# Zero-padding the keys' second parts to 128 rows in three attentions, and two runs of keys instead of three in the first

## The chip, the core and the metric

The kernel runs on one core of one Trainium2 chip. The metric is the device time of one execution in microseconds, the median of several runs. A core has a matrix engine (TensorE, PE in the rows; its weight loads are shown apart as PEld), a vector engine (VectorE, DVE), a scalar engine (ScalarE, ACT), a general engine (GpSimd, POOL) and SyncE (SP), whose queue issues most of the DMA transfers here. Each engine works through its own list of instructions in order; they wait for each other by semaphores.

## What is computed

Two transformer blocks on 1024 tokens of width 1024, with 256 context tokens beside them, in float32. The change touches the scores of all attentions. The first block has banded attention: 128 queries at a time see the tile of keys before, their own and the next one, and the context's 256 keys, with a sink; 8 query heads share 2 key heads of width 64.

```python
def latent_window_attention(q, k, v, kc, vc, sink):
    ...
    s_loc = jnp.einsum('bnqgrd,bnkgd->bngrqk', qb, kb).astype(jnp.float32) * scale
    s_ctx = jnp.einsum('bnqgrd,bcgd->bngrqc', qb, kc).astype(jnp.float32) * scale
    ...
    valid = (jnp.abs(i_pos - j_pos) <= WINDOW) & (j_pos >= 0) & (j_pos < L)
    s_loc = jnp.where(valid[None, :, None, None], s_loc, -jnp.inf)
    ...
    p = jax.nn.softmax(jnp.concatenate([s_loc, s_ctx, s_sink], axis=-1), axis=-1)
```

The second block has two layers, each with full attention of 4 heads over 1280 keys (1024 of the tokens, 256 of the context; in the first layer the context's queries see its own 256 alone). A key has 128 features of its own and 64 rotated ones that the heads share:

```python
def block_attention(q, k, v):
    ...
        s = jnp.einsum('bqhd,bkhd->bhqk', qblk, k).astype(jnp.float32) * scale
        p = jax.nn.softmax(s, axis=-1).astype(v.dtype)
        return jnp.einsum('bhqk,bkhv->bqhv', p, v)
```

## The kernel before

To keep float32 accuracy, an operand is split into a first part (rounded to the matrix engine's fast format) and a second part, what the rounding left; a product is made of three: first by first, first by second, second by first. Where only 64 features are contracted, two of these go into one product of 128 rows: `qs` holds the queries' first part in rows 0 to 63 and their second part in rows 64 to 127, `k1` holds the keys' first part twice. The third product, queries' first part by keys' second part `k2`, has only 64 rows.

**First block** (`attention1`, stage 361 to 633 us). Lines 1469 to 1492 transpose keys and queries and build `k1`, `k2` and `qs`. Then, for 8 tiles of 128 queries, 2 key heads and 4 query heads each, `scores` makes one score: a tile `S` of 128 queries by 512 or 640 keys in one of two buffers. It has runs of keys of 256 (context), 256 and, for 6 of the 8 query tiles, 128 columns; each run is a product by `k1` (L1507, 128 rows) and one by `k2` (L1508, 64 rows). The band masks are added by products of a unit matrix with `mr`, one per tile at the band's end (L1511). VectorE takes the maximum (L1513, L1514), ScalarE the exponentials (L1516); `normalise` scales them, `turn` transposes them on TensorE (L1536) and copies them out, `values` multiplies them with the values (L1546) and sends the result out (L1550). Between these run the steps of `fill`: modulations of later layers, whose weights `araw` come from DRAM through three buffers (DMA issues L120 and L177 on SP's queue, products L124 and L179 on 32 columns of the array each).

The order of this stage is not the order in the code: steps are recorded, and a scheduler of the framework sets the order on each engine when the program is built. At run time that order is fixed.

**Second block** (`layer`, twice: attention at 2527 to 2832 and 3815 to 4090 us). For each head `prep` makes the operands of the next head while `scores` works on this one: for 128 queries, `SA` takes 1024 keys in two runs of 512 columns, `SC` the context's 256. Each run is three products of the 128 features (`mm3`, L87 to L89), one by `k1` (L480, 128 rows) and one by `k2` (L481, 64 rows). Transposes (L511, L442, L449) and the products with the values (L87 to L89 into `tps`) stand between; `tps` has three buffers, which ScalarE and VectorE empty.

Of the kernel before, what the change touches and what calls it, by code (L numbers as in the profile page):

```python
# [9 lines left out]
F32R = mybir.dt.float32r  # L10
# [7 lines left out]
P = 128  # L18
# [6 lines left out]
def bc_rows(ap, n, extra=()):  # L25
    """DRAM vector read by every partition."""
    return bass.AP(tensor=ap.tensor, offset=ap.offset, ap=[[0, P]] + list(extra) + [[1, n]])


class Base:  # L30
# [23 lines left out]
    def rsqrt(self, pool, ss, n, scale, eps, out=None):  # L54
        """(ss * scale + eps) ** -0.5 of a [128, n] tile, by Newton's iteration."""
# [6 lines left out]
        # every step turns the sign  # L62
# [28 lines left out]
    # adaptive modulation -------------------------------------------------  # L91
    def ada_new(self, pool, pre, w_ap, bcol_ap, brow_ap, cc_ap, gates):
        """A modulation to be worked out by chunks; gates: {chunk: DRAM rows [2, 512]}."""
# [18 lines left out]
    def ada_steps(self, m, ap, pp, chunks, nk=2, bufs=3, pb=1):  # L112
        """One chunk a step."""
# [29 lines left out]
class Block2(Base):  # L143
# [10 lines left out]
    def mods2(self, l, ap, pp, bufs=3):  # L154
        """The modulation of a layer, in steps: rows of shifts, 1 + scales and gates.
        Every fourth of the columns goes through its own fourth of the array."""
# [32 lines left out]
    def mod_row(self, pool, l, w, i, n=1, name="mr", q=None, **kw):  # L189
        """n modulation rows from the i-th on every partition."""  # L190
        t = pool.tile([P, n, 1024], F32, name=name, **kw)
        (q or self.nc.sync).dma_start(t, bass.AP(tensor=self.mrow.tensor, offset=self.mrow[w, l, 1024 * i:].offset, ap=[[0, P], [1, 1024 * n]]))
        return t

    def norm(self, srcs, A, B, sp, pp, sink, rows=None, between=None, xbufs=2, copy=None):
        """srcs: list of (dram [n,1024] or SBUF [128,T,1024], first tile, tiles, which); sink(k, tok0, n, f32 tile).
        between: run after the rows are scaled; copy: engine of each scaled copy of SBUF rows."""
# [39 lines left out]
    # ---------------------------------------------------------------------  # L237
    def layer(self, l, xin, cin, xmid, cmid, hn, hnc, ready=False, crows=None):
        """xmid, cmid: the rows after this layer; hn, hnc: room for modulated rows;
        ready: its modulation is worked out; crows: the context's modulated rows, if they are. the experts are chosen."""  # L240
# [13 lines left out]
    def mixers(self, l, last, lp, xin, cin, crows):  # L254
# [27 lines left out]
        # ---- the input projection, by tiles of tokens  # L282
        with self.pool(f"w{l}") as wp, self.pool(f"wps{l}", space=PSUM) as pp:
# [15 lines left out]
            def weights(c0, cn):  # L299
                """A step splits a piece; the second parts go where the pieces split before were loaded."""  # L300
# [19 lines left out]
            # rows are scaled two tiles ahead of their products, and transposed one ahead  # L320
# [40 lines left out]
        # ---- what attention keeps  # L361
        hp = s_mix.enter_context(self.pool(f"hd{l}"))
        tps = s_mix.enter_context(self.pool(f"tps{l}", space=PSUM))
        # the rotated shared part of the keys
# [5 lines left out]
        def head_set(pool):  # L370
            t = lambda n, s, d=F32R: pool.tile(s, d, name=n)
            return dict(kth=t("kth", [P, 1280]), ktl=t("ktl", [P, 1280]), k1=t("k1", [P, 1280]), k2=t("k2", [64, 1280]),
                        qth=t("qth", [P, NQ]), qtl=t("qtl", [P, NQ]), qs=t("qs", [P, NQ]),
                        vh=t("vh", [P, 10, P]), vl=t("vl", [P, 10, P]), rq=t("rq", [P, 10], F32))
        sets = [head_set(hp)]
# [13 lines left out]
        def prep(h, S):  # L389
            """The operands of one head, in steps."""  # L390
# [45 lines left out]
            for T, src, srcr, sc, dh, dl, d1 in ((10, kn, krh, kncol, S["kth"], S["ktl"], S["k1"]), (TQ, qn, qrr, qncol, S["qth"], S["qtl"], S["qs"])):  # L436
                for g0 in range(0, T, 4):
# [14 lines left out]
                    if d1 is S["k1"]:  # L452
                        nc.scalar.copy(d1[64:128, o], fl)
                        nc.vector.tensor_tensor(S["k2"][:, o], fl, asf(d1[0:64, o]), op=OP.subtract)
# [8 lines left out]
        # ---- attention, one head's operands ahead  # L463
        hb = s_mix.enter_context(self.pool(f"hb{l}"))
        sets.append(head_set(hb))
        with self.pool(f"at{l}") as ap, self.pool(f"atps{l}", space=PSUM) as pp:
# [4 lines left out]
            def scores(u):  # L471
                """Unnormalised probabilities of 128 queries."""
# [4 lines left out]
                for out, k0, n in ([(SA[:, :512], 0, 512), (SA[:, 512:], 512, 512)] if SA is not None else []) + [(SC, 1024, 256)]:  # L477
# [3 lines left out]
                    nc.tensor.matmul(out, S_["qs"][0:64, q], S_["k2"][:, kk], start=False, stop=True)  # L481
# [75 lines left out]
    def rope2(self, dst, g, tmp):  # L557
        """dst [128, 8, 64] <- rotated g; they may be the same."""
# [10 lines left out]
    def ctx_rows(self, pool):  # L569
        """The context's rows as the first layer's input projection takes them."""  # L570
# [8 lines left out]
    def rows_in(self, x, ab, wp, fast=False):  # L579
        """The norm and the modulation of one tile of tokens."""  # L580
# [9 lines left out]
    def turn_in(self, x, wp, pp):  # L590
        """Features on partitions, as two parts."""
# [9 lines left out]
    def project_in(self, t, only_kv, h, fin, wp, pp, W, cqh, cql, ckh, ckl, kr, sskr, f, u2, gv, ssv, qln, kvln):  # L601
        """One tile of tokens: the projection, and what follows it row by row; returns the last step, fin is the last tile's."""
# [49 lines left out]
    def spatial(self, l, last, TQ, f, u2, gv, ssv, sgun, bsg):  # L652
        """Spatial gating and Fourier mixing."""
        nc, ins = self.nc, self.ins
        with self.pool(f"g{l}", side="right") as cp, self.pool(f"gps{l}", space=PSUM) as pp:
            def piece(k, o, n):
                """Room for n tokens from o of the k-th features, and the way to their place."""
# [16 lines left out]
            # Fourier: the tokens  # L674
# [30 lines left out]
            # the gate  # L705
# [7 lines left out]
            # Fourier: the features  # L713
# [45 lines left out]
    def project(self, l, last, xin, cin, xmid, cmid, hn, hnc, ep):  # L759
        """The output projection, the rows' second norm, and the choice of every expert's rows.  # L760
        Returns the steps of the choice that are left."""
# [5 lines left out]
        with self.pool(f"r{l}", side="right") as rp, self.pool(f"rps{l}", space=PSUM) as pp:  # L767
            with self.pool(f"o{l}") as op_:
                # all the weights are on their way before there is room for their parts
# [19 lines left out]
                def turn(U):  # L789
                    """The router's view of a tile, and its affinities with those of the tiles before it."""  # L790
# [13 lines left out]
                def cat(c):  # L804
                    """The features of a tile."""
# [4 lines left out]
                def router(mr):  # L810
                    """The router's weights with the norm's scales, and what its shifts add."""
# [103 lines left out]
    def route(self, rp, pp, U, af, o, tag, bufs=2):  # L915
        """Affinities of two tiles of tokens, experts on partitions from o."""
# [29 lines left out]
    def choose(self, w, T, cap, rp, pp, ep, af, tag, bufs=2):  # L946
        """The cap tokens of largest affinity of every expert, and their affinities.
        Many tokens go in two halves, sorted beside each other: of the i-th of one and the i-th last of the other
        the larger one is among the cap largest of both."""
# [48 lines left out]
    def experts(self, l, last, xmid, cmid, hn, hnc, ep, af):  # L998
        """Every expert's rows, weighted and gated, added to the rows they came from."""
# [1225 lines left out]
```

## Time and profile before

| | us |
|---|---|
| median of 3 runs | 4630.02 |
| lowest and highest run | 4618.53 and 4631.8 |
| span of the profiled execution | 4613.0 |
| TensorE busy in that span | 4229.6 (92 %) |
| VectorE busy | 2803.5 (61 %) |
| ScalarE busy | 1835.0 (40 %) |
| GpSimd busy | 1057.6 (23 %) |

The page gives the profiled execution's own time as its span from the first to the last instruction; what lies around the span has no row. The three stages that the change touches are 852 us of it. A matrix product's end is modelled in such a profile, its start is not: how close products follow is read from the starts. Times in rows are microseconds from the span's start.

### The profile page before, as it was taken

The page shows a single profiled execution, that of the slowest core. Times are in us where ns is not written, and L with a number is a line of the kernel's source. Part 1 is how long each engine was busy: PE and PEld are TensorE (multiplying, and loading weights), DVE is VectorE, ACT ScalarE, POOL GpSimd, SP SyncE. Part 2 cuts the span into 40 slices and gives each one's busy share as a digit, 9 for nine tenths or more (in the row PEclk, how much of TensorE's full clock was granted, in tenths as well). Part 3 has the DMA queues.
Part 4 walks back from the last instruction along what each step waited for, and adds up shares of the span by engine and source line. Part 5 has one row for each costly group of instructions (what it writes and reads, how often), then busy time and mean ns, then how long its engine had stood idle before and what let it go on. Part 6 is the DMA issues. An engine that isn't in the chain of part 4 may idle for free. (4 is left out here: it accounts for less than half of the span.)

```text
span 4613.0 us, 70037 instructions
## 1 busy us (share of the span) xinstructions
PE 4229.6 (92%) x27212; PEld 3189.4 (69%) x27212; DVE 2803.5 (61%) x5419; ACT 1835.0 (40%) x3590; POOL 1057.6 (23%) x863
## 2 busy tenths in 40 slices
PE   7998999999799999999897999889998889995988
PEld 6874567777667888889786777544444767774776
DVE  5365557677686544445655665655555656656888
ACT  4233234444433211212344664144443436641665
POOL 1000012222131201100211212433342202224564
PEclk9999989899999999999898999899999889997999
DMA  6226635555562322220302013467776110135996
GB/s 230 68 87 200 206 102 127 148 124 126 106 204 90 127 86 92 92 79 27 122 19 77 13 46 122 147 202 227 216 222 190 67 57 18 53 107 198 317 349 213
DMA packets 433204, 611.92 MB, mean 133 GB/s; under 512 B 93888, under 2 KB 259920, under 8 KB 431976
## 3 DMA queue, kind: packets, MB, share of 16 engines
q1 hardware_dynamic: 403800, 527.74, 35.8%
q0 software_dynamic: 29072, 79.70, 6.6%
q8 instruction: 214, 3.51, 0.3%
q14 instruction: 118, 0.97, 0.1%
HBM read 510.29 MB, written 97.05 MB: 132 GB/s over the span
## 5 line engine op out<-in xcount | busy, mean ns | idle before, releaser
L1024 DVE TENSOR_TENSOR wl<-raw,wh 128x1024 fp32r<-128x1024 f32 x284 | 402.6, 1464 | 129.3 <-ACT wh L1023 127.2
L1023 ACT CAST wh<-raw 128x1024 fp32r<-128x1024 f32 x384 | 390.0, 1052 | 184.3 <-PE pg L89 107.2
L1024 POOL TENSOR_TENSOR wl<-raw,wh 128x1024 fp32r<-128x1024 f32 x100 | 257.6, 2582 | 420.1 <-ACT wh L1023 382.2
L87 PE MATMUL pu<-z,uh 128*128 128x256 f32 x1024 | 293.7, 287 | 4.6 <-ACT uh L77 4.6
L89 PE MATMUL pu<-z,ul 128*128 128x256 f32 x1024 | 291.1, 284 | 2.3 <-DVE ul L78 2.3
L88 PE MATMUL pu<-hl,uh 128*128 128x256 f32 x1024 | 291.0, 284 | 0.0
L2057 DVE TENSOR_TENSOR x<-x,pd 128x512 f32<-128x512 f32 x256 | 174.3, 686 | 128.2 <-PE pd L89 128.2
L87 PE MATMUL gps<-wh,hh 128*128 128x512 f32 (+2 forms) x656 | 225.5, 344 | 18.1 <-ACT hh L77 13.1
L2029 POOL TENSOR_TENSOR raw<-raw,g 128x1024 f32<-128x1024 f32 x32 | 82.1, 2580 | 638.5 <-DMA raw<-w_mlp_down 455.3
L89 PE MATMUL gps<-wh,hl 128*128 128x512 f32 (+2 forms) x656 | 222.4, 340 | 1.2 <-POOL hl L1356 1.0
L87 PEld LDWEIGHTS pu<-z,uh 128*128 128x128 f32 x1024 | 197.6, 193 | 14.8 <-issue 5.3
L87 PE MATMUL pd<-dh,ah 128*128 128x512 f32 x512 | 200.1, 391 | 2.2 <-DVE x L2057 2.0
L88 PE MATMUL pd<-dl,ah 128*128 128x512 f32 x512 | 199.6, 390 | 0.0
L89 PE MATMUL pd<-dh,al 128*128 128x512 f32 x512 | 199.5, 390 | 0.0
L89 PEld LDWEIGHTS pu<-z,ul 128*128 128x128 f32 x1024 | 197.4, 193 | 2.6 <-DVE ul L78 2.6
L88 PEld LDWEIGHTS pu<-hl,uh 128*128 128x128 f32 x1024 | 197.6, 193 | 0.1
L1062 PE MATMUL pcx<-raw,xc 128*32 128x256 f32 x1024 | 160.4, 392 | 0.0
L77 ACT CAST wh<-raw 128x512 fp32r<-128x512 f32 (+1 forms) x120 | 73.5, 614 | 203.2 <-PE gp L88 85.7
L87 PEld LDWEIGHTS gps<-wh,hh 128*128 128x128 f32 x656 | 130.8, 200 | 32.2 <-ACT hh L77 14.3
L77 ACT CAST dh<-raw 128x1024 fp32r<-128x1024 f32 x32 | 32.2, 1048 | 282.3 <-PE pd L89 276.2
L89 PEld LDWEIGHTS gps<-wh,hl 128*128 128x128 f32 x656 | 130.7, 200 | 15.0 <-POOL hl L1356 1.5
L2046 DVE TENSOR_TENSOR r<-r 128x512 f32<-128x512 f32 x64 | 54.1, 845 | 142.2 <-ACT ah L2045 142.2
(676 smaller groups left out, 12226.7 us busy)
## 6 DMA issues: line engine op xcount, KB each, us to landing
araw<-w_ada SPq DMA_DIRECT2D x144, 512.0 KB
raw<-w_gate SPq DMA_DIRECT2D x128, 512.0 KB
raw<-w_up SPq DMA_DIRECT2D x128, 512.0 KB
raw<-w_down SPq DMA_DIRECT2D x128, 512.0 KB
raw<-w_in SPq DMA_DIRECT2D x100, 256.0 KB
raw<-w_mlp_up SPq DMA_DIRECT2D x32, 512.0 KB
raw<-w_mlp_down SPq DMA_DIRECT2D x32, 512.0 KB
x<-x SPq DMA_DIRECT2D x24, 512.0 KB
```

The costliest lines, as they stand in the source:

```text
L77: nc.scalar.copy(hi, src)
L87: mm(ps, lh, rh, start=start, stop=False)
L88: mm(ps, lh, rl, start=False, stop=False)
L89: mm(ps, ll, rh, start=False, stop=stop)
L1023: nc.scalar.copy(h, raw)
L1024: (nc.gpsimd if ahead or i % 4 == 3 else nc.vector).tensor_tensor(lo, raw, asf(h), op=OP.subtract)
L1062: nc.tensor.matmul(out[32 * (j0 + g):32 * (j0 + g) + 32, :], xc, w[:, 256 * g:256 * g + 256], start=start, stop=stop, tile_position=(0, 32 ...
L2029: nc.gpsimd.tensor_tensor(raw2, raw2, g2, op=OP.mult)
L2046: nc.vector.tensor_tensor(r, r, r, op=OP.mult)
L2057: nc.vector.tensor_tensor(x[:, t, s], x[:, t, s], p, op=OP.add)
```

## The change

The tiles `k2` get 128 rows. The lower half is filled as before; rows 64 to 127 are set to zero once by GpSimd. The product by `k2` then takes all 128 rows of `qs`: the queries' second part meets zeros, so the sum is the same. This is done in the first block and in both layers of the second (two sets of operands each).

In the first block a score has two runs: the near tiles of keys in one (384 or 256 columns, ending at column 512 of `S`) and the context (256 columns from column 512 on). The two band masks of a middle tile of queries are added in one product, whose output takes the first and the third tile of the near run. The tiles' order in the probabilities changes with that: near tiles first, context last. Comments are removed too.

```diff
@@ layer
-            return dict(kth=t("kth", [P, 1280]), ktl=t("ktl", [P, 1280]), k1=t("k1", [P, 1280]), k2=t("k2", [64, 1280]),
+            return dict(kth=t("kth", [P, 1280]), ktl=t("ktl", [P, 1280]), k1=t("k1", [P, 1280]), k2=t("k2", [P, 1280]),
...
-        sets = [head_set(hp)]
+
+        def padded(S):
+
+            nc.gpsimd.memset(asf(S["k2"][64:128]), 0.0)
+            return S
+        sets = [padded(head_set(hp))]
...
-                        nc.vector.tensor_tensor(S["k2"][:, o], fl, asf(d1[0:64, o]), op=OP.subtract)
+                        nc.vector.tensor_tensor(S["k2"][0:64, o], fl, asf(d1[0:64, o]), op=OP.subtract)
...
-        sets.append(head_set(hb))
+        sets.append(padded(head_set(hb)))
...
-                    nc.tensor.matmul(out, S_["qs"][0:64, q], S_["k2"][:, kk], start=False, stop=True)
+                    nc.tensor.matmul(out, S_["qs"][:, q], S_["k2"][:, kk], start=False, stop=True)
@@ attention1
-            k2 = ap.tile([64, 2, 1280], F32R, name="k2")
+            k2 = ap.tile([P, 2, 1280], F32R, name="k2")
+            nc.gpsimd.memset(asf(k2[64:128]), 0.0)
...
-                    nc.vector.tensor_tensor(k2[:, g, o], f[own], asf(k1[own, g, o]), op=OP.subtract)
+                    nc.vector.tensor_tensor(k2[0:64, g, o], f[own], asf(k1[own, g, o]), op=OP.subtract)
...
-                segs = [(0, 256, 1024), (256, 256, lo * P)] + ([(512, NK - 512, lo * P + 256)] if NK > 512 else [])
-                for c, n, k0 in segs:
-                    st = c != 256
-                    o, kk = slice(c, c + n), slice(k0, k0 + n)
-                    nc.tensor.matmul(S[:, o], qs[:, h, q], k1[:, g, kk], start=st, stop=False, skip_group_check=True)
-                    nc.tensor.matmul(S[:, o], qs[0:64, h, q], k2[:, g, kk], start=False, stop=False, skip_group_check=True)
-                for i, tl in enumerate(tiles):
-                    if tl == b - 1 or (tl == b + 1 and tl < 8):
-                        nc.tensor.matmul(S[:, i * P:i * P + P], idr, mr[:, 0 if tl < b else 1], start=False, stop=True, skip_group_check=True)
+
+                n = NK - 256
+                a = 512 - n
+                for o, kk in ((slice(a, 512), slice(lo * P, lo * P + n)), (slice(512, 768), slice(1024, 1280))):
+                    near = o.start < 512
+                    nc.tensor.matmul(S[:, o], qs[:, h, q], k1[:, g, kk], start=True, stop=False, skip_group_check=True)
+                    nc.tensor.matmul(S[:, o], qs[:, h, q], k2[:, g, kk], start=False, stop=not near, skip_group_check=True)
+                    if near and n == 384:
+                        ends = S[:, a:512].rearrange("p (t k) -> p t k", k=P)[:, 0::2]
+                        nc.tensor.matmul(ends, idr, mr, start=False, stop=True, skip_group_check=True)
+                    elif near:
+                        i = 1 if b == 0 else 0
+                        nc.tensor.matmul(S[:, a + i * P:a + i * P + P], idr, mr[:, i], start=False, stop=True, skip_group_check=True)
+                S = S[:, a:768]
...
-                nc.vector.tensor_reduce(mx, S[:, :NK], axis=AX.X, op=OP.max)
+                nc.vector.tensor_reduce(mx, S, axis=AX.X, op=OP.max)
...
-                nc.scalar.activation(pr[:, :NK], S[:, :NK], AF.Exp, scale=0.125, bias=nm[:, r:r + 1], accum_out=rs[:, r:r + 1])
+                nc.scalar.activation(pr[:, :NK], S, AF.Exp, scale=0.125, bias=nm[:, r:r + 1], accum_out=rs[:, r:r + 1])
...
-                tiles = [8, 9] + list(range(lo, hi))
+                tiles = list(range(lo, hi)) + [8, 9]
```

On TensorE the order of the second block's layers stays word for word; in the first block's attention it moves. There, in the latter half of the stage, a score, the modulation behind it (`aps<-araw`) and the first transpose stood like this before (a row is line, operation, output<-inputs with buffer numbers, output rows x columns):

```order
L1507 MATMUL S_4424<-k1_2955,qs_2957 128x256
L1508 MATMUL S_4424<-k2_2956,qs_2957 128x256
L1507 MATMUL S_4424<-k1_2955,qs_2957 128x256
L1508 MATMUL S_4424<-k2_2956,qs_2957 128x256
L1507 MATMUL S_4424<-k1_2955,qs_2957 128x128
L1508 MATMUL S_4424<-k2_2956,qs_2957 128x128
L1511 MATMUL S_4424<-mr_2960,idr_2962 128x128 x2
L179 MATMUL aps_4222<-araw_4438,msc_3428 32x256 x4
L1536 MATMUL tps_4448<-ident_60,pr_4218 128x128
```

Now, at the matching place, between two modulations (L1514, L1515 and L1518 are the products by `k1`, by `k2` and of the masks, L1547 the transposes):

```order
L179 MATMUL aps_4148<-araw_4320,msc_3426 32x256 x4
L1514 MATMUL S_4527<-k1_2955,qs_2958 128x384
L1515 MATMUL S_4527<-k2_2956,qs_2958 128x384
L1518 MATMUL S_4527<-mr_2961,idr_2963 128x2x128
L1514 MATMUL S_4527<-k1_2955,qs_2958 128x256
L1515 MATMUL S_4527<-k2_2956,qs_2958 128x256
L1547 MATMUL tps_4544<-ident_60,pr_4385 128x128
L1547 MATMUL tps_4544<-ident_60,pr_4412 128x128
L1547 MATMUL tps_4544<-ident_60,pr_4435 128x128
L179 MATMUL aps_4148<-araw_4343,msc_3426 32x256 x4
```

A score is five products instead of eight, and about one score still stands between two modulations.

On SP's queue, towards the end of that stage, the modulations' weights (`araw`) stood like this before, beside weights of the next stage (L1268), rows of finished modulations (L186, L173) and the attention's results (L1550):

```order
L177 DMA araw<-w_ada 128x1024 x2
L1268 DMA raw<-w_in 128x4x128
L177 DMA araw<-w_ada 128x1024
L1268 DMA raw<-w_in 128x4x128
L177 DMA araw<-w_ada 128x1024
L1550 DMA yad<-yo 512x1x128
L177 DMA araw<-w_ada 128x1024 x4
L186 DMA mrow_3422<-mrw 4x256 x2
L173 DMA mbr<-b_ada 4x256 x2
L177 DMA araw<-w_ada 128x1024 x4
L1550 DMA yad<-yo 512x1x128
```

Now, at the matching place (L1273 is the next stage's weights, L1561 the attention's results):

```order
L177 DMA araw<-w_ada 128x1024 x2
L1561 DMA yad<-yo 512x1x128
L177 DMA araw<-w_ada 128x1024 x6
L186 DMA mrow_3420<-mrw 4x256 x2
L173 DMA mbr<-b_ada 4x256 x2
L177 DMA araw<-w_ada 128x1024 x2
L1561 DMA yad<-yo 512x1x128
L177 DMA araw<-w_ada 128x1024 x4
L1273 DMA raw<-w_in 128x4x128 x3
L186 DMA mrow_3420<-mrw 4x256 x2
```

The loads of `araw` stand in longer runs, and the next stage's weights behind them instead of between them.

On GpSimd's queue the first block's zeros (L1464) stand behind the last step of the input projection (`u`) and ahead of the clears for the recurrence (`TT`, `SV`), which is the stage after attention:

```order
L1415 MEMSET u 128x1 x2
L1415 MEMSET u 128x2
L1415 MEMSET u 128x1
L1464 MEMSET k_2956 64x2560
L1722 MEMSET TT 32x8x32 x6
L1762 MEMSET SV 64x256 x2
L1722 MEMSET TT 32x8x32 x2
```

The row of L1464 is new there, the others stood in this order before. In the second block a memset of 64x1280 stands behind the first step of the key rotation (L367) in each layer, and one ahead of the `ones` for the row sums.

## Rows read from the trace of the kernel before

**Rows 1.** Busy time by stretches: us from:to, length, each engine (instructions), granted clock, DMA share, GB/s:
```profile
361.00:633.00 272.00, 269.05 (x1466) 143.04 (x1467) 149.57 (x328) 80.38 (x189) 0.61 (x2) 0.96 0.57 178
2527.00:2832.00 305.00, 297.24 (x1814) 232.52 (x1812) 185.90 (x452) 185.24 (x497) 69.30 (x92) 0.99 0.11 36
3815.00:4090.00 275.00, 268.81 (x1615) 208.79 (x1616) 164.33 (x394) 160.74 (x432) 53.45 (x69) 0.99 0.11 38
432.00:434.00 2.00, 2.00 (x7) 0.48 (x5) 0.72 (x1) 0.00 (x0) 0.00 (x0) 0.53 0.23 51
4350.00:4400.00 50.00, 46.84 (x216) 37.07 (x215) 49.67 (x38) 36.17 (x42) 26.57 (x13) 1.00 1.00 352
```

**Rows 2.** Timeline, TensorE, second block's first layer: start, duration, engine, line, what, idle:
```profile
2648.55 0.39 PE L89 MATMUL SA<-kth,qtl 128*128 128x512 f32 x1
2648.55 0.19 PEld L480 LDWEIGHTS SA<-k,qs 128*128 128x128 f32 x1
2648.78 0.40 PE L480 MATMUL SA<-k,qs 128*128 128x512 f32 x1
2649.10 0.18 PEld L481 LDWEIGHTS SA<-k,qs 64*128 64x128 f32 x1 [0.36 <-issue]
2649.10 0.50 PE L481 MATMUL SA<-k,qs 64*128 64x512 f32 x1
2649.53 0.39 PE L87 MATMUL SC<-kth,qth 128*128 128x256 f32 x1
...
2649.76 0.28 PE L88 MATMUL SC<-ktl,qth 128*128 128x256 f32 x1
2649.88 0.28 PE L89 MATMUL SC<-kth,qtl 128*128 128x256 f32 x1
2649.99 0.28 PE L480 MATMUL SC<-k,qs 128*128 128x256 f32 x1
2650.20 0.38 PE L481 MATMUL SC<-k,qs 64*128 64x256 f32 x1
```

**Rows 3.** Timeline, TensorE, one score of five tiles in the first block:
```profile
541.15 0.36 PE L1507 MATMUL S<-k,qs 128*128 128x256 f32 x1
541.45 0.38 PE L1508 MATMUL S<-k,qs 64*128 64x256 f32 x1
541.76 0.38 PE L1507 MATMUL S<-k,qs 128*128 128x256 f32 x1
...
542.38 0.33 PE L1507 MATMUL S<-k,qs 128*128 128x128 f32 x1
542.64 0.32 PE L1508 MATMUL S<-k,qs 64*128 64x128 f32 x1
542.89 0.44 PE L1511 MATMUL S<-mr,idr 128*128 128x128 f32 x2
543.26 0.64 PE L179 MATMUL aps<-araw,msc 128*32 128x256 f32 x8
```

**Rows 4.** The line of the 64-row product, both layers: durations ns, starts, rows*columns:
```profile
L481 PE MATMUL SA<-k,qs x128: 491/500/503, 2530.5 to 4085.4; 64*128 64x512 f32 x128
L481 PE MATMUL SC<-k,qs x72: 378/381/384, 2532.9 to 4086.5; 64*128 64x256 f32 x72
```

**Rows 5.** The line of the first block's 64-row product:
```profile
L1508 PE MATMUL S<-k,qs x176: 322/381/580, 361.7 to 632.5; 64*128 64x256 f32 x128, 64*128 64x128 f32 x48
```

**Rows 6.** SP's queue, 340 to 660 us: its waits, and one line's issues:
```profile
SPq L177 <- PE aps L179: 60.3, 28, 6.5
SPq L120 <- PE aps L124: 47.3, 19, 5.8
L177 SPq DMA_DIRECT2D araw<-w_ada x48: 327/328/571, 445.8 to 599.7; - x48
```

**Rows 7.** Groups on VectorE, 361 to 633 us: busy us, mean ns, idle before:
```profile
L1513 DVE TENSOR_REDUCE mx<-S 128x1 f32<-128x640 f32 (+1 forms) x63 | 49.7, 790 | 72.0 <-PE S L1511 71.9
```

**Rows 8.** Groups on GpSimd, 2300 to 2860 us:
```profile
L766 POOL MEMSET af<- 48x512 f32 x1 | 0.5, 543 | 0.0
```

More of the change, by code (lines that the diff above doesn't have):

```diff
@@ L1493, in scores @@
             def scores(u, r):
-                g, b, lo, NK, tiles = u["g"], u["b"], u["lo"], u["NK"], u["tiles"]
+                g, b, lo, NK = u["g"], u["b"], u["lo"], u["NK"]
                 q = slice(b * P, b * P + P)
```

## The prediction

> **What bounds the kernel now.** I read the busy time by stretches first, for the three stages that the change touches: the first block's attention (361 to 633 us) and the attention of the second block's two layers (2527 to 2832 and 3815 to 4090) [rows 1]. In all three TensorE is busy nearly throughout (269.05 of 272.00, 297.24 of 305.00, 268.81 of 275.00), while VectorE stands at 149.57, 185.90 and 164.33 and ScalarE lower still. So the set of TensorE's instructions sets these stages. But a busy TensorE need not be moving columns, so I read the timeline next, and there not the durations but the distances from one start to the next: where products follow each other without a gap, that distance is what one costs.
>
> In the second block [rows 2] a 128-row product of 512 columns starts 0.23 us after the one before it (2648.55 to 2648.78), one of 256 columns 0.11 to 0.12 us (2649.76, 2649.88, 2649.99). Its weight load is hidden: that of L480 starts at 2648.55, together with the product ahead of it. Around the 64-row product L481 this breaks. Its load starts only at 2649.10, with its own product: 0.32 us after the start of L480 and not 0.23. The 128-row product that follows starts 0.43 us later, not 0.23, and the next one 0.23 us after that, though it is of 256 columns, where 0.12 would do. So a 512-column product on 64 rows costs 0.09 + 0.20 + 0.11 = 0.40 us more than the same product on 128 rows. With 256 columns the way in is 0.21 (2649.99 to 2650.20), 0.09 too much; the way out is 0.31 against 0.12, read in the first block (541.45 to 541.76) [rows 3], 0.19 too much; and with the 0.11 behind it the sum is 0.39.
>
> **The change part by part. Second block.** The products keep their number and columns, only the rows grow. There are 128 such products of 512 columns and 72 of 256 [rows 4]: 128 x 0.40 + 72 x 0.39 = 51 + 28 = 79 us. Some of them stand next to a transpose instead, where less is to be had; I take 77 (bounds 70 and 80). What is late next: the softmax's and the transposes' evacuations on VectorE and ScalarE, whose work stays as it is. VectorE's 185.90 us would then stand in about 266, 70 per cent against 61. That is not a bound, but TensorE's few waits for free transposing buffers will grow. I charge 10 us for both layers (0 to 25): 67 us net.
>
> **First block, TensorE.** A score of five tiles of keys is six products and two masks; from its first start to the first instruction behind it 541.15 to 543.26 = 2.11 us [rows 3]. There are 64 scores: 48 with three runs and 16 with two, which give the 176 64-row products [rows 5]. One of two runs has four distances of 0.31 and one mask of about 0.18, together 1.42. Before: 48 x 2.11 + 16 x 1.42 = 124 us. After, every one of the five products is on 128 rows. One of 384 columns stands nowhere in the trace; between 0.12 for 256 and 0.23 for 512 I take 0.17. Undisturbed that is 0.17 + 0.17 + 0.12 + 0.12 + 0.12 = 0.70. Where a score is followed by products of the modulations (32 columns of the array), its last one, now of 256 columns, can cost up to the 0.31 seen on the way out of a 64-row one, so 0.70 to about 0.97 with smaller switches; in the new order TensorE's scores stand broken up by transposes, modulations and values as before, so I take 0.90, and 0.80 for one of two runs. After: 48 x 0.90 + 16 x 0.80 = 56 us. Saved 124 - 56 = 68 us (64 to 81). The merged mask is in that sum: one distance of 0.12 for two.
>
> **First block, what comes late next.** (a) The modulations' weights. They come through three buffers, and the new order hardly changes how many scores stand between two of them, so they are wanted a quarter sooner. Today it is the queue that waits for TensorE, 60.3 + 47.3 = 108 us [rows 6], more than the 68 saved, and the DMA engines are 0.57 busy [rows 1]: 272 x 0.57 = 155 us of transfers against some 204 us. On average they fit; in bunches they do not always. I charge 8 us (0 to 25). (b) VectorE has 149.57 us to do in 204 instead of 272, 73 per cent; its reduction takes 0.79 us and waits 72 us for scores today [rows 7], which is the reserve. Two scores in a row without other work will wait for one of the two score buffers: 5 us (0 to 15).
>
> **The zeros.** Five memsets on GpSimd. The nearest row is 0.54 us for 512 elements a partition [rows 8]; by elements 1280 take about 1.4 and 2560 about 2.7. Cover: GpSimd works 0.61 us in the first block's whole stage [rows 1], and behind the memset there its queue holds only clears for the stage after. In the second block the memsets stand ahead of the key rotation and ahead of the ones for the row sums, in a queue that is 69.30 of 305.00 busy. I take 0; with no cover 4 x 1.4 + 2.7 = 8 us. The recurrence behind the first block's attention is ordered a little differently; nothing in the trace prices that: 0, give or take 5.
>
> **Sum.** 67 + 68 - 8 - 5 = 122 us. Does it reach the end? Behind the last attention the experts' weights stream at full DMA share (1.00 at 4350 to 4400) [rows 1], but DMA is at 0.11 in the attention before it, so this stream is held by buffers and starts with the stage: it moves along. The profiled span of 4613.0 us becomes 4491. The median of the runs is 4630.02, 17.0 above that span; I carry the difference over: 4508 us.
>
> **Rivals.** *No new waits*: all 77 + 68 = 145 us come through, 4485. For it: VectorE and ScalarE have 30 per cent in reserve everywhere. Against it: TensorE's order is fixed, so every late buffer stops it.
>
> *The weights hold the first block back*: if the loads keep today's pace, the last is issued at 599.7 as now [rows 6], and only the last 33 of 272 us shrink: 68 x 33 / 272 = 8 us, and with the second block's 67 that is 75, 4555. For it: three buffers, and a queue in which other transfers stand between the loads. Against it: the 108 us in which it waits for TensorE.
>
> *Padding gains nothing*: the extra distances belong to the position, not to the 64 rows. Then only the merging pays: per score of three runs 542.38 to 542.89 (0.51 us) and one mask of 0.16 go, 2 x 0.06 come for the wider run: 0.56 x 48 = 27 us, 4603. The load of L480 at 2648.55 beside a product on the same 128 rows speaks against it. The Trainium skill (TensorE: Matmul & The Clock Gate, The mechanism) speaks for it: there a weight load overlaps a running matmul only when it goes to another row group, so a padded product would wait for its load just as well, and the result would be this 4603. The row of L480 shows a hidden load on the same rows, so I give the rule little.
>
> *Slower by the clock*: at 432 to 434 the granted clock is 0.53 though TensorE is busy throughout [rows 1]. If the first block's stage, with denser products and more short waits, fell to the lower level, 1.2 GHz, for most of its length, its 204 us at 0.96 would stretch; it eats the whole 122 us when it reaches 326, that is at a mean of 0.96 x 204 / 326 = 0.60. All of it at 0.5: 392 us, so 4508 + 188 = 4696. Against it: the mean is 0.96 in this stage and 0.99 in the others, with the same neighbours.
>
> **How the numbers follow.** Forecast 0.67 (4480 to 4535 by its own bounds), no new waits 0.13, weights hold 0.12, padding gains nothing 0.05, slower by the clock 0.03. The range of 4478 to 4556 takes in the first three, with the unknown waits at their far ends. Three per thousand, some 14 us, is about what a measurement can tell from no change: faster 0.95, same 0.02, slower 0.03.
>
> **What would show it.** In the profile after, a product of L1515 and of L481 should start 0.12 to 0.24 us after the one before it, its load beside that product. The stretches of attention should be about 39 and 35 us shorter less a few (second block) and 55 us (first). TensorE's waits for araw, S and tps show what was given back; if the queue's wait for aps has gone to zero, the weights hold. If the distances stay at 0.31 and 0.43, padding gained nothing and the forecast is wrong; if a stage's granted clock is near 0.6, likewise.

## The result, and the profile after

The changed kernel takes 4511.24 us (median of 4 runs, 4499.0 to 4516.1), the kernel before 4626.55 us beside it: a ratio of 0.9752 (95 per cent interval 0.973 to 0.9773). Predicted were 4508 us, between 4478 and 4556. The profiled execution has a span of 4507.5 us, that of before 4613.0. The page gives the busy time of the engines (share of the span, instructions); TensorE, PE, was busy for 4229.6 us before, the others hardly change:

```profile
PE 4110.9 (91%) x27068; PEld 3166.0 (70%) x27068; DVE 2800.4 (62%) x5419; ACT 1833.0 (41%) x3590; POOL 1067.8 (24%) x868
```

The three stages first, by the view of busy time by stretches. Each goes from the start of its first score product to the start of its last score product, in the first block to that of its last value product: the 633 us of [rows 1] is where the last scores start, while the last values start at 643.1. Columns: from:to, length, TensorE, its weight loads, VectorE, ScalarE, GpSimd, granted clock, DMA share, GB/s. Before:

```profile
361.30:643.00 281.70, 278.46 (x1513) 149.02 (x1514) 154.88 (x342) 84.33 (x198) 0.61 (x2) 0.96 0.56 174
2527.60:2811.50 283.90, 280.75 (x1716) 219.27 (x1714) 172.90 (x431) 171.85 (x475) 62.33 (x84) 1.00 0.09 32
3818.00:4086.50 268.50, 262.35 (x1575) 203.05 (x1573) 160.89 (x385) 156.70 (x424) 53.45 (x69) 1.00 0.11 39
```

After, the same three:

```profile
358.90:573.70 214.80, 207.07 (x1364) 111.31 (x1365) 151.01 (x340) 83.51 (x195) 0.61 (x2) 0.99 0.70 226
2471.00:2725.00 254.00, 247.66 (x1716) 219.10 (x1715) 170.62 (x431) 170.44 (x475) 62.46 (x84) 0.99 0.11 35
3733.60:3973.70 240.10, 228.00 (x1575) 202.52 (x1574) 159.85 (x385) 155.96 (x424) 53.56 (x69) 1.00 0.13 43
```

The first block's stage is 66.9 us shorter, the layers' 29.9 and 28.4. These are 125.2 us, but the spans differ by 105.5: some 20 us were lost outside the three stages, 11 of them in the recurrence behind the first and 7 behind the second layer's attention, from its last product to the end of the span (526.5 before, 533.8 after). In the second and third line the other engines have nearly the same work as before, and TensorE, idle for 3 and 6 us before, is now idle for 6 and 12.

The timeline of TensorE in the first layer, at a place like that of [rows 2] (start, duration, engine, line, what):

```profile
2516.44 0.39 PE L89 MATMUL SA<-kth,qtl 128*128 128x512 f32 x1
2516.67 0.40 PE L485 MATMUL SA<-k,qs 128*128 128x512 f32 x1
2516.91 0.39 PE L486 MATMUL SA<-k,qs 128*128 128x512 f32 x1
2517.14 0.28 PE L87 MATMUL SC<-kth,qth 128*128 128x256 f32 x1
2517.25 0.28 PE L88 MATMUL SC<-ktl,qth 128*128 128x256 f32 x1
...
2517.49 0.28 PE L485 MATMUL SC<-k,qs 128*128 128x256 f32 x1
2517.61 0.28 PE L486 MATMUL SC<-k,qs 128*128 128x256 f32 x1
2517.73 0.39 PE L87 MATMUL SA<-kth,qth 128*128 128x512 f32 x1
```

L486 is the padded product. It starts 0.24 us after L485, the next starts 0.23 us after it and the one behind that 0.11; [rows 2] had 0.32, 0.43 and 0.23. The weight load of L486 has its own row, and it starts at 2516.67, together with the product ahead of it:

```profile
2516.67 0.19 PEld L486 LDWEIGHTS SA<-k,qs 128*128 128x128 f32 x1
```

One score in the first block, the counterpart of [rows 3], and the first two products of the next one:

```profile
471.85 0.44 PE L1514 MATMUL S<-k,qs 128*128 128x384 f32 x1
472.12 0.34 PE L1515 MATMUL S<-k,qs 128*128 128x384 f32 x1
472.30 0.28 PE L1518 MATMUL S<-mr,idr 128*128 128x256 f32 x1
472.42 0.28 PE L1514 MATMUL S<-k,qs 128*128 128x256 f32 x1
472.54 0.28 PE L1515 MATMUL S<-k,qs 128*128 128x256 f32 x1
472.75 0.64 PE L179 MATMUL aps<-araw,msc 128*32 128x256 f32 x8
473.32 0.44 PE L1514 MATMUL S<-k,qs 128*128 128x384 f32 x1
473.60 0.34 PE L1515 MATMUL S<-k,qs 128*128 128x384 f32 x1
```

From the first start to the first instruction behind it: 0.90 us, where [rows 3] had 2.11. The 384 columns cost 0.18 from L1515 to the masks (0.17 was assumed), but 0.27 and 0.28 from L1514 to L1515, behind a transpose and behind a modulation.

### The profile page after: what moved, and what is told of

Read it like the earlier page. It is cut to its first block, busy times and chain, and to the rows that moved or that the text cites. A ratio compares the mean times of both kernels' runs of the same rounds, so it can differ in the third digit from the quotient of the medians.

```text
span 4507.5 us, 69748 instructions
## 1 busy us (share of the span) xinstructions
PE 4110.9 (91%) x27068; PEld 3166.0 (70%) x27068; DVE 2800.4 (62%) x5419; ACT 1833.0 (41%) x3590; POOL 1067.8 (24%) x868
```

## The experiments

Ratios are against runs of the kernel before on the same chip, with 95 per cent intervals. Where a few microseconds matter, I go by the lengths of stages in the profiles, with the same bounds as above. The layers' two stages together came out between 551.4 and 552.5 us in four profiles with the old layers and between 492.5 and 495.3 in six with the new ones, so they can be trusted to about 3 us. The first block's stage took 281.7, 277.7 and 280.3 us in three profiles with the old first block, at a granted clock between 0.96 and 0.98, and between 214.8 and 218.6 in five with the new one, at 0.99: there 4 us are scatter.

**One part at a time: the layers.** `attention1` as before; of the diff only the part in `layer`.

> Only the second block's part: k2 of the two layers on 128 rows, the first block's attention as before. Account by switches: the two layers get shorter as in the changed kernel, 30 + 28 = 58 us, nothing moves ahead of them (the recurrence at 633 to 906 us takes as long as before, with its dips of the clock in the same places), and some 5 us are given back in the last stage: ratio about 0.9875, span about 4557. If the parts did not add (the layers' gain partly being the first block's), the layers' stages would shorten by clearly less than 58. Rival, position and not rows: no change, ratio 1.000.

Measured: 0.9882 (0.986 to 0.9904), 55 us by the ratio and 53 by the medians. The stages are 253.7 and 240.1 us, 58.6 together shorter: the gain is the layers' own. But the recurrence did not stay as it was: it took 10 us more than in the profile of before, though nothing ahead of it had changed.

**The first block alone.** `layer` as before, `attention1` as changed.

> Only the first block's part: two runs, merged mask, k2 on 128 rows there; the layers as before. Account: the stage from the first S to the last po gets 67 us shorter. Theory A, the 14 us that the changed kernel lost again in the recurrence behind it belong to this part (the low stretches of the granted clock fall otherwise when the recurrence is ordered and timed as here): 67 - 14 = 53 us, ratio about 0.9885. Theory B, they were chance of one execution: 67 us, ratio about 0.9855, and the profile of this run shows the recurrence with the dips of before.

Measured: 0.9859 (0.9834 to 0.9883), 65 us by the ratio and 69 by the medians; the stage 216.7 us, 65.0 shorter. The recurrence lost 3 us here, with the first block of the changed kernel ahead of it. This is what theory B gives; the 0.9885 of theory A lies just outside the interval. The two parts together give 0.0118 + 0.0141 = 0.0259, some 120 us, and the changed kernel 0.0248 and, further down, 0.0279: they add, as far as the intervals can tell. The part behind the second layer's attention took 533.0 us here and 532.6 and 532.7 in the next two runs, though the layers of all three are those of before: the 526.5 in the profile of before was a short execution of it, and the 7 us above are not the change's.

**The runs and masks without the padding.** On top of the kernel before:

```diff
-                segs = [(0, 256, 1024), (256, 256, lo * P)] + ([(512, NK - 512, lo * P + 256)] if NK > 512 else [])
...
+                n = NK - 256
+                a = 512 - n
+                for o, kk in ((slice(a, 512), slice(lo * P, lo * P + n)), (slice(512, 768), slice(1024, 1280))):
...
+                    nc.tensor.matmul(S[:, o], qs[0:64, h, q], k2[:, g, kk], start=False, stop=not near, skip_group_check=True)
...
+                        nc.tensor.matmul(ends, idr, mr, start=False, stop=True, skip_group_check=True)
```

> The first block's two runs and merged mask, but k2 on 64 rows everywhere. Account by switches: a score of five tiles goes from 2.11 us to about 1.42 + 0.12 for the wider run, 0.57 less, 48 of them 27 us in the stage; with up to 14 us lost again in the recurrence the ratio is 0.994 to 0.997. Rival, padding gains nothing and the merging all: 67 us in the stage, ratio 0.9855 to 0.9885 as with padding.

**The padding without the runs and masks.** On top of the kernel before:

```diff
-            k2 = ap.tile([64, 2, 1280], F32R, name="k2")
+            k2 = ap.tile([P, 2, 1280], F32R, name="k2")
+            nc.gpsimd.memset(asf(k2[64:128]), 0.0)
...
-                    nc.tensor.matmul(S[:, o], qs[0:64, h, q], k2[:, g, kk], start=False, stop=False, skip_group_check=True)
+                    nc.tensor.matmul(S[:, o], qs[:, h, q], k2[:, g, kk], start=False, stop=False, skip_group_check=True)
```

> The first block's k2 on 128 rows with three runs and two masks as before; the layers as before. Account by switches: a score of five tiles goes from 2.11 us to 4 x 0.12 + 2 x 0.11 + 2 x 0.11 = 0.92 and some 0.1 to 0.2 at its end, 1.1; 48 x 1.0 + 16 x 0.6 = 58 us in the stage; less up to 14 in the recurrence, ratio 0.9875 to 0.9905. Together with the run that merges alone this says how much the two overlap (27 + 58 against 67). Rival, position and not rows: no change, ratio 1.000.

Measured: the runs and masks alone 0.993 (0.9904 to 0.9956), the stage 248.8 us, 32.9 shorter; the padding alone 0.989 (0.9867 to 0.9914), 230.0 us, 51.7 shorter. Expected were 27 and 58. The two stages as stretches, the runs and masks first:

```profile
359.20:608.10 248.90, 244.73 (x1365) 118.96 (x1365) 152.85 (x341) 83.85 (x196) 0.61 (x2) 0.99 0.61 195
```
```profile
363.50:593.60 230.10, 214.26 (x1514) 123.83 (x1514) 153.56 (x342) 84.28 (x198) 0.61 (x2) 1.00 0.66 212
```

With the padding alone TensorE is idle for 16 us in this stage, twice as long as in the changed kernel. Both parts together took 65.0 off, so they overlap by 20 us. A part of each figure is the clock, 0.96 in the stage of before: an estimate by length times granted clock (unrounded) gives 271.5 us before, 245.4, 229.9, and 215.0 for both together, that is 26, 42 and 57 saved and an overlap of 11. A run less removes two changes between 64 and 128 rows, and the padding removes the same changes. Ranked by what each adds to the other, the padding is worth 32 us (248.8 to 216.7) and the runs and masks 13 (230.0 to 216.7), with the clock taken out 30 and 15. That padding gains nothing is refuted twice, here and in the layers.

**Is it the 64 rows, or the change of rows?** The kernel before, but in the layers the three 64-row products of a score stand together:

```diff
                     nc.tensor.matmul(out, S_["qs"][:, q], S_["k1"][:, kk], start=False, stop=False)
-                    nc.tensor.matmul(out, S_["qs"][0:64, q], S_["k2"][:, kk], start=False, stop=True)
+                for out, k0, n in ([(SA[:, :512], 0, 512), (SA[:, 512:], 512, 512)] if SA is not None else []) + [(SC, 1024, 256)]:
+                    nc.tensor.matmul(out, S_["qs"][0:64, q], S_["k2"][:, k0:k0 + n], start=False, stop=True)
```

> The kernel before, with k2 on 64 rows everywhere, but in the two layers the three 64-row products of a score stand together at its end instead of one behind each run. Account by switches (what costs is going from 128 to 64 rows and back): two of three switches of a score go, 2 x 0.40 us in 64 scores = 51 us of nominal time, some 10 of it given back in waits as with the padding, so about 41: ratio 0.991 (0.989 to 0.994 if the inner loads are not all hidden). Rival, every 64-row product is dear by itself: ratio 1.000.

Measured: 0.9932 (0.9909 to 0.9956); the stages 266.7 and 254.0 us, 31.7 shorter. The 64-row products are all still there, so it is the change. It is less than the 41 expected, which were 51 less 10 for waits: the scheduler kept all three together in only 42 of the 64 scores, and two of them in 19 more. That leaves 97 places where 64-row products are entered, not 200, and 103 x 0.40 makes 41 us instead of 51; 9 of these came back, 7 of them as waits in TensorE's rows for transposing buffers (9.0 us before, 16.3 here). The timeline of TensorE shows one group and what follows it:

```profile
2619.73 0.28 PE L89 MATMUL SC<-kth,qtl 128*128 128x256 f32 x1
2619.84 0.28 PE L480 MATMUL SC<-k,qs 128*128 128x256 f32 x1
2620.05 0.73 PE L482 MATMUL SA<-k,qs 64*128 64x512 f32 x2
2620.62 0.28 PE L482 MATMUL SC<-k,qs 64*128 64x256 f32 x1
2620.83 0.50 PE L87 MATMUL SA<-kth,qth 128*128 128x512 f32 x1
2621.17 0.39 PE L88 MATMUL SA<-ktl,qth 128*128 128x512 f32 x1
2621.39 0.39 PE L89 MATMUL SA<-kth,qtl 128*128 128x512 f32 x1
```

Into the group 0.21 us instead of 0.12: 0.09 too much. Its first two products together take 0.57 instead of 0.46: the second starts 0.11 late (0.337 us in the middle of 50 such pairs), the third does not. Out of it 0.21 instead of 0.12, 0.09 again, and the product behind that starts 0.34 after, not 0.23: 0.11 again. So **each change of rows, in either direction, costs 0.20 us: 0.09 before the first product behind it and 0.11 before the second.** Three products together pay 0.40, as one alone did.

**The changed kernel twice more**, for the 20 us lost outside the stages.

> The changed kernel once more, with another profile. Theory A, the 14 us lost in the recurrence come from how this kernel times it: the granted clock is again 0.60 behind 820 us and the offset to the kernel before goes again from -69 to -55. Theory B (for which the runs of one part alone speak): the low stretches fall elsewhere in every execution: the offset behind the recurrence comes out by 5 us or more otherwise, and the ratio of the medians lies nearer to the sum of the parts, 0.974.

> The changed kernel a third time, as the base for the run beside it and for the scatter of the recurrence: if its length goes with its granted clock alone (length times clock 331 to 334 us in ten profiles so far, 358 us at 0.93 to 371 at 0.89), it does so here too, wherever this one falls; the first block's stage again 215 to 217 us, the two layers together 494.

Measured: 0.9721 (0.9697 to 0.9744) and 0.9721 (0.9691 to 0.9751), medians 4499.98 and 4502.92 us, some 130 us below before. The first block's stage is 216.2 and 218.6 us, near the 214.8 of the first profile (215 to 217 was expected of the last), and the layers take 493.8 and 492.5, but the recurrence behind it is not repeated. Busy time by stretches from the same first to the same last instruction of VectorE there, columns as above: before, the changed kernel, again, and a third time:

```profile
645.00:1005.00 360.00, 326.25 (x3592) 256.92 (x3590) 254.32 (x666) 161.08 (x351) 84.50 (x119) 0.92 0.57 141
```
```profile
578.97:950.31 371.34, 337.78 (x3588) 267.37 (x3586) 253.58 (x666) 161.18 (x351) 82.94 (x114) 0.89 0.55 137
```
```profile
583.50:941.93 358.43, 322.60 (x3592) 254.91 (x3590) 253.36 (x666) 161.64 (x351) 84.28 (x114) 0.93 0.58 142
```
```profile
584.04:958.07 374.03, 340.47 (x3588) 269.44 (x3586) 253.90 (x666) 161.34 (x351) 83.13 (x114) 0.88 0.55 136
```

The same work takes between 358.43 and 374.03 us in three executions of one kernel, and length times granted clock is nearly one number: 331, 330, 333 and 329 (331 to 334 was expected of the last). Over all twelve profiles it is 328 to 334, and the length does not go with the change: 360.0, 370.0 and 365.5 us behind the old first block, 358.4 to 374.0 behind a changed one. Where the loss sits in the first of them is seen in 20 us of it; the second line is the matching place when the kernel ran again:

```profile
824.00:844.00 20.00, 20.00 (x286) 17.22 (x283) 4.78 (x9) 12.22 (x28) 2.55 (x5) 0.50 0.31 88
```
```profile
816.00:836.00 20.00, 18.94 (x325) 15.64 (x323) 6.28 (x11) 12.39 (x29) 4.68 (x8) 0.81 0.42 115
```

At 824 to 844 TensorE ran at the lower of its two levels, 1.2 GHz, throughout, while it was busy throughout; why it fell there is not shown. So the loss in the recurrence belongs to an execution and not to the change. Theory B holds for it; what was expected of the total, a ratio nearer to 0.974, was passed on the other side, at 0.9721.

**Two and four buffers for the modulations' weights** instead of three, in the changed kernel.

```diff
-                fill = chain(self.ada_steps(m1, ap, pp, range(4, 12), bufs=3), *(j(ap, pp) for j in jobs))
+                fill = chain(self.ada_steps(m1, ap, pp, range(4, 12), bufs=2), *(j(ap, pp, bufs=2) for j in jobs))
```

For four, the same with `bufs=4`, and in `attention1`:

```diff
-            mk = self.load(ap, "bandm", [P, 2, P])
+            mk = ap.tile([P, 4, P], F32, name="yo", bufs=1)[:, :2]
+            nc.sync.dma_start(mk, ins["bandm"])
...
-                yo = ap.tile([P, 4, P], F32, name="yo", bufs=2)
+                yo = ap.tile([P, 4, P], F32, name="yo", bufs=1)
```

> The changed kernel with two buffers instead of three for the modulations' weights (araw) in the first block's attention. If the weights are near the limit there, as the 8 us charged for them (0 to 25) assumed, one buffer less costs 20 us or more in that stage (ratio 0.980 or above). Rival, the ring has slack, since the queue still waits 77 us for TensorE to free a buffer: under 8 us, ratio 0.975 to 0.977.

> The changed kernel with four buffers instead of three for the modulations' weights (araw) in the first block's attention; the room comes from yo, one buffer instead of two, which the band masks share. With three buffers TensorE waits some 8 us there for araw (weight loads 6.5, products 1.5), and with two the stage took 17 us more. If the ring is what keeps those 8 us, the stage gets 4 to 8 us shorter than the 215 to 217 of the changed kernel, ratio about 0.001 to 0.002 below it. Rival, the transfers themselves are late (DMA share 0.70) and the weights just as late: no shorter; or the single yo costs a wait of TensorE for po and it is 1 to 5 us longer.

TensorE's weight loads waiting for a transfer of `araw` (waits: who, for whom, us, times, longest), 340 to 600 us, in the changed kernel, with two buffers and with four:

```profile
PEld aps L179 <- DMA araw<-w_ada: 6.5, 11, 1.1
```
```profile
PEld aps L179 <- DMA araw<-w_ada: 20.4, 23, 3.6
```
```profile
PEld aps L179 <- DMA araw<-w_ada: 1.5, 3, 0.8
```

Two buffers: 0.9765 (0.974 to 0.979), the stage 233.1 us, 17 more, at a granted clock of 0.96 instead of 0.99, and the modulations that are left over delay the start of the recurrence by some 9 more in the profile; the median is 18 us above that of the changed kernel beside it. The 17 us lie between the two expectations. (The ratio falls into the rival's range, but that was reckoned from 0.9752, and the changed kernel beside it stood at 0.9721.) One buffer less costs something; whether three have slack is the question of the run with four. Four buffers: 0.972 (0.9697 to 0.9742) beside 0.9721, no difference, and the stage takes 216.6 us, no less. The waits for the weights are nearly gone, and no row shows a wait for the single `yo`, but another one grew from 6.1 us to this in the stage (waits of the weight loads, four buffers; this kernel's lines stand one lower there: L1528 is the exponential, L1515 the product by `k1`):

```profile
PEld S L1515 <- ACT pr L1528: 10.2, 12, 2.1
```

TensorE, earlier at its scores, finds the score buffer not yet read by ScalarE. The 8 us were not to be had by this, so three buffers are enough here.

**The layers' waits.** In the changed kernel TensorE waits in the layers for `tps`, held by ScalarE's squares of the queries. The squares taken from the copy in SBUF instead:

```diff
-                    nc.scalar.activation(junk, ps[:, i, :192], AF.Square, accum_out=ssq[:, 2 * g + i:2 * g + i + 1])
+                    nc.scalar.activation(junk, qn[:, 2 * g + i], AF.Square, accum_out=ssq[:, 2 * g + i:2 * g + i + 1])
```

> The changed kernel, but in the layers the squares of the queries are taken from their copy in SBUF and not from PSUM, so that the PSUM buffer tps comes free after the copy and not after two squares more. Account: the padding's 15 us of new waits in the layers are TensorE waiting for tps, mostly behind this line (4.1 + 6.8 us in the first layer, 4.7 + 7.4 in the second, PE and its weight loads, partly the same time): the two stages get 8 to 20 us shorter than in the changed kernel, ratio about 0.972 to before. Rival, the next release of tps (VectorE's subtractions) is just as late: no shorter, ratio 0.975.

Measured: 0.9744 (0.9719 to 0.9769), no gain, and the two stages take 500.1 us, 6 more. TensorE's waits in the first layer, the changed kernel and this one (L529 is VectorE's output of the values, L429 the copy):

```profile
PE tps L516 <- ACT junk L431: 4.1, 6, 0.9
PE tps L516 <- DVE yo L529: 1.1, 2, 0.6
```
```profile
PE tps L516 <- DVE yo L529: 5.3, 3, 1.9
PE tps L516 <- ACT qn L429: 4.8, 9, 0.7
```

The wait for the squares is gone, and waits for the copy itself and for VectorE stand in its place. The scheduler also put some of TensorE's products and transposes in another order here, so which of the two made the 6 us stays open.

## Why the prediction came out right, step by step

| step | predicted, us | measured, us |
|---|---|---|
| layers: changes of rows | -77 | -73 |
| layers: more waits | +10 | +15 |
| first block: scores | -68 | -64 |
| first block: more waits | +13 | +5 to +9 |
| recurrence | 0 (5 either way) | +11, -2, +14 in three profiles |
| sum | -122 | -115, -130, -131 (medians) |

The last row is not the sum of the measured terms, which without the recurrence make -113 to -117. It compares medians; and the first block's stage of before ran at a lower clock, so that the three stages as they ran shrank by 125.

*How near it came.* That 4508 lies 3 us from 4511.24 is in part luck. The forecast span was 4491, and the profiled one 4507.5; the 17 us added for the median, most of which the section on the recurrence below puts down to a short execution of before, made up for it. The two later medians, 4499.98 and 4502.92, are 130 us under before, so the net saving of 122 was rather too small. The mechanism and the order of its terms were right.

*Layers.* Counted over all starts into, out of and behind the padded products, the distances shrank by 38.3 and 35.0 us, 0.37 for each of the 200 where 0.40 and 0.39 were read. The stages shrank by 58.3, so 15 us came back. Nine of them stand in TensorE's own rows of waits (9.0 us in both layers before, 17.9 after), nearly all for transposing buffers, as was said; the other six have no row of their own, though waits of the weight loads for the same buffers grew too. The largest are in the second layer, these two rows, before 3.7 and 2.2 us,

```profile
PE tps L516 <- ACT junk L431: 4.7, 3, 1.8
PE tps L87 <- DVE ptl L78: 3.9, 3, 1.3
```

and 2.7 us for VectorE's `yo` (L529), which was no wait before.

*First block, scores.* All distances behind its products and masks sum to 125.4 us before (predicted 124) and 61.8 after (predicted 56). The term that was too small is a score's surroundings. That its last product costs more ahead of a modulation was in the 0.90 us (0.21 from 472.54 to 472.75, where up to 0.31 was allowed); that the first product behind a modulation or a transpose is dear too was not: 0.28 from 473.32 to 473.60 and 0.27 from 471.85 to 472.12, some 0.10 too much. In the 48 scores with 384 columns that is up to 5 us of the 6.

*First block, new waits.* 13 us were charged, and the stage shrank by more than the scores did. Part of this is the clock: the stage of before was read at 0.96; with the same first block it took 277.7 us at 0.98 in the run of the layers alone. Length times clock (unrounded) is 272 and 273 there and 213 to 217 in five profiles with the new first block, 55 to 59 less, against the 64 of the scores: by this estimate 5 to 9 us of waits. The rows agree with the two causes that were named: in the stage the weight loads wait 8.3 us for transfers of `araw`, 1.0 before, and 6.1 us for a score buffer that ScalarE has yet to read, 2.5 before. The expected reserves were there. VectorE's reduction, 72 us of waiting for scores in [rows 7], has 28.6 of them left:

```profile
L1524 DVE TENSOR_REDUCE mx<-S 128x1 f32<-128x640 f32 (+1 forms) x64 | 50.2, 786 | 29.0 <-PE S L1515 28.6
```

SP's queue, 108 us of waiting in [rows 6], has these left:

```profile
SPq L120 <- PE aps L124: 42.5, 20, 4.4
SPq L177 <- PE aps L179: 34.9, 27, 2.2
```

77 us, so the weights do not hold the stage; with two buffers 17 of its 67 us are lost again.

*Zeros.* The memsets take 2.2 us in the first block and 2.3 us in each layer (two of them), near the estimate, and no engine waits for them (SP's queue once, for 0.3 us):

```profile
L1464 POOL MEMSET k<- 64x2560 f32 x1 | 2.2, 2234 | 13.9 <-DVE cv L1425 13.9
```

*Recurrence.* The step that failed in its size: the order there was given 5 us either way, but what moves is the clock, and by 16 us from one execution to the next. It makes 11 of the 20 us by which the difference of the two spans, 105.5, falls short of the stages' 125. The forecast's base had the same scatter in it: the profiled span of before was 17 us under its median, of which 1.8 lies around the span in the later runs' records; the rest was a short execution (the times of before lie between 4610.93 and 4644.71).

*Rivals.* Padding gains nothing: the loads of L486 and the two runs of one part refute it, and with it the rule of the Trainium skill (TensorE: Matmul & The Clock Gate, The mechanism) as it was read there. Another section of the same page (Step-by-step: what each phase is for) says that weights may also be loaded ahead into a background buffer. The row at 2516.67, a load beside a product on the same 128 rows, agrees with that; the buffer itself no run shows. Slower by the clock: the granted clock in the first block's stage was 0.99. No new waits and weights hold lie on either side of what came.

## What to carry to other kernels

Read TensorE's price from the distance between starts, not from durations. If a product on fewer rows stands alone among full ones, count the changes of rows, 0.20 us each here: fill the rows with zeros, or put such products together. Before a gain in one stage is judged from two spans, take the stage's own length and its granted clock: here the layers' stages repeated to 3 us and the first block's to 4, while the spans of one kernel moved by 12.

## What the runs showed of the hardware that was not expected

A change of rows delays two products, not one: 0.09 us before the first and 0.11 before the second, 0.20 in all, also among 64-row products after they were entered (0.337 us from the first to the second, 0.235 from there to the third). About the same price shows at other steps, where the rows stay at 128: from a score's product to a modulation on 32 columns 0.21 us instead of 0.12, and 0.28 instead of 0.18 from the first product behind it to the second. The number of columns alone does not explain it, as behind a transpose, which has 128 like the score, the second product is late too (0.27 instead of 0.18, from 471.85 to 472.12); the cause stays open. And the granted clock of the recurrence differs between executions of one kernel (0.88 to 0.93), with TensorE at 1.2 GHz for 20 us at a stretch while it was busy throughout.
